# FoX attention block: the chunk factors of the softmax from four ScalarE activations instead of a GpSimd subtraction and one activation

## The chip, the cores and the metric

One core of a Trainium2 chip runs the whole program. The time is the device time of one execution in microseconds (us). The kernel before takes 590.53 us, the median of three runs (589.92 to 590.91). Lower is better.

The engines carry these names in the profile: PE is TensorE (matmuls and transposes), PEld its weight load, DVE is VectorE, ACT is ScalarE, POOL is GpSimd, SP only starts transfers. Each engine takes its instructions in order, and an instruction that waits holds up everything behind it on its engine.

## The reference

The input is 1024 positions of width 1024, with 16 learned positions put ahead of them (1040 in all). One layer does this, in float32:

```python
u    = rmsnorm(h, norm_g)
proj = u @ w_in     # q, k, v, forget logit, SiLU gate z, and four 512-wide parts of a convolution branch
c    = cumsum(log_sigmoid(f_logit + b_f))
s[t, j] = q_t . k_j / 8 + c[t] - c[j]   for j <= t, else -inf       # 8 heads of 64
attn = softmax(s) @ v
y    = concat(group_rmsnorm(attn) * silu(z), group_rmsnorm(gate_b * conv3(gate_c * xc)) * silu(z_conv))
out  = rmsnorm(h + y @ w_out, final_norm_g)[16:]
```

The change concerns the softmax. A row of scores is handled in two or three chunks of keys. Each chunk is exponentiated against its own maximum and summed; later each chunk is multiplied by exp(chunk maximum - row maximum) / (row sum).

## The kernel before

Float32 matmuls are done as three matmuls on split operands (high times high, low times high, high times low); `whi`/`wlo`, `ph`/`pl` and the like are such pairs. The first 160 us hold the projections to q, k, v and the forget logits. From about 160 to 490 us two streams are woven together on PE: the attention of eight heads, and as filler the remaining projection blocks (line 165, tile `pj`). From 490 us comes the output projection (line 788).

Each head is done in two halves of four 128-row query tiles: the narrow half (`c` = 0, tiles 0 to 3, up to 528 keys) and the wide half (`c` = 1, tiles 4 to 7, up to 1040 keys). For a half:

- `s_step` (lines 597 to 614), once per query tile and chunk: PE makes scores in `pn` (lines 605, 606); DVE takes the negated chunk maximum into `nmx` (line 612, or line 609 with the causal mask); ACT writes exp(score - maximum) into the SBUF tile `pn` of the row, with the sum into `smx` (line 613).
- `s_end` (lines 616 to 636), once per half, so 16 times: DVE reduces `nmx` to `mx`, the negated row maximum (619). POOL forms `mx - nmx` (621) and ACT exponentiates it (622): these are the factors `e`, 12 numbers in each of the 128 rows. POOL makes the row sums (624, 626, 627), DVE their reciprocal (628), POOL the final factors `fc` (630), and then multiplies each chunk of `pn` by its factor (635), nine pieces in a wide half and five in a narrow one.
- `t_step` (638 to 660): PE transposes 128-key slices of `pn` into `pt` (645); for slices on the diagonal DVE also fills a 32-wide corner (649, 651). ACT copies `pt` to `ph` (654), DVE makes the remainder `pl` (115).
- `v_step` (669): PE multiplies `ph` and `pl` by the values into `po`; `fold` (680, 681) takes them out.

The first transposes of a half need the first chunk of all four query tiles, that is the first four pieces of line 635. I number the 16 executions of `s_end` in order of time: odd ones end a wide half, even ones a narrow half. End 1 is at 177 us, end 3 at 216, end 7 at 295, end 9 at 336, end 10 at 354, end 11 at 375 and end 15 at 454.

The filler blocks each need a 128 x 1024 weight tile split in two: POOL copies `wm` to `wmhi` (line 112), and DVE makes `wmlo` from both (line 115). `wmhi` has two buffers, so a copy can start only when PE has read the last of the block before the present one.

The matmuls of the woven part are held in program order (`pinned`). All else is ordered by a scheduler that runs a timeline model over the program, so a change of one instruction's modelled time or engine can move others on ACT, DVE and POOL.

Of the kernel before, what the change touches and what calls it, by code (L numbers as in the profile page):

```python
# [11 lines left out]
AF = mybir.ActivationFunctionType  # L12
ALU = mybir.AluOpType
# [4 lines left out]
P = 128  # L18
# [17 lines left out]
def hybrid_kernel(ctx, tc, hT, h, w_q, w_vf, w_m, w_o, gn, bf, cw, ga, gc, gf, out):  # L36
    nc = tc.nc
# [141 lines left out]
    with ExitStack() as ca:  # L179
# [73 lines left out]
        for b in range(3):  # L253
            pr = psx.tile([P, 512], F32, name="px")
            w = 512 if b < 2 else NM
            for i in range(4 if b < 2 else 1):
                j = 4 * b + i
# [311 lines left out]
    nmx, smx = [], []  # L569
# [46 lines left out]
    def s_end(c):  # L616

        mx = pnp.tile([P, 4], F32, name="mx")
        nc.vector.tensor_reduce(mx, nmx[c], AX.X, ALU.min)
        e = pnp.tile([P, 4, 3], F32, name="e")  # L620
        nc.gpsimd.tensor_tensor(e, mx.unsqueeze(2).broadcast_to([P, 4, 3]), nmx[c], ALU.subtract)
        nc.scalar.activation(e, e, AF.Exp)
        t = pnp.tile([P, 4, 3], F32, name="t")
        nc.gpsimd.tensor_mul(t, e, smx[c])
        s = pnp.tile([P, 4], F32, name="s")
        nc.gpsimd.tensor_add(s, t[:, :, 0], t[:, :, 1])
        nc.gpsimd.tensor_add(s, s, t[:, :, 2])
        nc.vector.reciprocal(s, s)
        fc = pnp.tile([P, 4, 3], F32, name="fc", bufs=2)
        nc.gpsimd.tensor_mul(fc, e, s.unsqueeze(2).broadcast_to([P, 4, 3]))  # L630
        for i in range(3):
            for j in range(4 * c, 4 * c + 4):
                if i < len(SCH[j]):
                    k0, w = SCH[j][i]
                    nc.gpsimd.tensor_scalar(pn[j][:, k0:k0 + w], pn[j][:, k0:k0 + w], fc[:, j % 4, i:i + 1], 1.0,  # L635
                                            ALU.mult, ALU.mult)
# [79 lines left out]
    for g in range(-1, 2 * HEADS):  # L716
        steps = []
        if g >= 0 and g % 2 == 0 and g // 2 + 1 < HEADS:
            steps.append((0.0, 0.0, lambda hd=g // 2 + 1: load_head(hd)))
        if g + 1 < 2 * HEADS:  # L720
            hd, c = (g + 1) // 2, g % 2
            todo = [(2 * SCH[j][i][1] / 2400.0, lambda hd=hd, j=j, i=i: s_step(hd, j, i))
                    for j in range(4 * c, 4 * c + 4) for i in range(len(SCH[j]))]
            lo, hi = S_AT[g % 2 if g >= 0 else 2]
            spread(steps, todo, lo, hi)
            steps.append((hi, WAIT[g % 2 if g >= 0 else 2], lambda c=c: s_end(c)))
        if g >= 0:
            hd, c = g // 2, 1 - g % 2
            box = {}
            tv = []  # L730
            nk = 4 * c + 5
            for kt in range(nk + V_LAG):
                if kt < nk:
                    w = 512 - max(0, (kt - 4 * c) * P - 32)
                    tv.append((w / 1200.0, lambda c=c, kt=kt, box=box: t_step(c, kt, box)))
                if kt >= V_LAG:
                    w = 512 - max(0, (kt - V_LAG - 4 * c) * P - 32)
                    tv.append((w / 1200.0, lambda hd=hd, c=c, kt=kt - V_LAG, box=box: v_step(hd, c, kt, box)))
            spread(steps, tv, T_AT[c], V_END)
            steps.append((0.99, 0.0, lambda hd=hd, c=c, box=box: fold(hd, c, box)))  # L740
            if g > 0 and (g - 1) % 4 >= 2:
                steps.append((0.05, SOON, lambda m=(g - 1) // 4, c=g % 2: finish_soon(m, c)))
        stages.append([(x, s) for _, x, s in sorted(steps, key=lambda t: t[0])])
# [164 lines left out]
```

## Time and profile before

| | |
|---|---|
| median of 3 runs | 590.53 us |
| profiled execution | 590.42 us, its span 588.6 us, granted PE clock 0.998 |
| PE busy | 575.7 us, 98% of the span |
| PEld busy | 508.9 us, 86% |
| DVE busy | 373.5 us, 63% |
| ACT busy | 285.3 us, 48% |
| POOL busy | 145.2 us, 25% |

Busy time is the sum of an engine's instruction times without overlaps. The span runs from the first instruction to the last; about 1.8 us of the execution's time lie outside it. A number in square brackets at the end of a row of the timeline is the idle time of the engine just before that instruction, with what released it. Matmuls overlap, and their ends are modelled, so a wait of PE shows fully only when it is longer than this overlap; a wait of PEld shows when the weights for the next matmul could be loaded.

### The profile page before, as it was taken

What the parts mean: (1) busy time and instruction counts of PE and PEld (TensorE: products, weight loads), DVE (VectorE), ACT (ScalarE), POOL (GpSimd) and SP (SyncE); (2) the same over time, 40 slices, a digit from 0 to 9 for tenths busy, and PEclk for the clock granted to TensorE, in tenths of its full rate; (3) what the DMA queues carried; (4) which work ended last, traced back from release to release, by engine and by line L of the source; (5) the groups of instructions that cost most, each with busy time, mean ns of one, the idle gap of its engine ahead of it and who ended that gap; (6) DMA issues with size and microseconds to landing.
All of it is one profiled execution on the core that took longest, in us unless ns stands there. A gap on an engine that the chain in (4) does not pass through costs nothing.

```text
span 588.6 us, 9150 instructions
## 1 busy us (share of the span) xinstructions
PE 575.7 (98%) x3230; PEld 508.9 (86%) x3230; DVE 373.5 (63%) x842; ACT 285.3 (48%) x667; POOL 145.2 (25%) x282
## 2 busy tenths in 40 slices
PE   9999999999998999999999999999999999999995
PEld 6889999999997889997879997888997878888884
DVE  5515951133356786879876878876879768847342
ACT  5354431131043574565763755756645657815231
POOL 1102010121027234242263155350531520000000
PEclk9999999999999999999999999999999999999999
DMA  8664694249811514514326126152251045743201
GB/s 296 215 223 135 207 339 139 71 144 282 257 53 37 146 36 116 141 59 114 86 77 145 55 94 146 63 130 66 80 211 37 1 162 225 240 161 128 88 36 71
DMA packets 35221, 78.14 MB, mean 133 GB/s; under 512 B 4024, under 2 KB 13384, under 8 KB 35176
## 3 DMA queue, kind: packets, MB, share of 16 engines
q1 hardware_dynamic: 35032, 77.57, 42.1%
q8 instruction: 25, 0.41, 0.3%
q14 instruction: 20, 0.16, 0.1%
q10 hardware_dynamic: 144, 0.00, 0.0%
HBM read 55.92 MB, written 21.64 MB: 132 GB/s over the span
## 4 chain that ended last, share of the span: by engine, by line
PE 83%; DVE 5%; DMA 4%; POOL 4%; ACT 2%; issue 1%; SPq 0%; POOLq 0%; ACTq 0%; DVEq 0%
PE pj L165 30%; PE p L788 10%; PE ps L324 8%; PE ps L232 7%; PE po L669 5%; PE pj L788 5%; PE pt L645 5%; PE ps L165 4%; DMA k<-kd 3%; PE pn L605 3%; PE pn L606 3%; POOL pn L635 1%; DMA wm<-in_w_m 1%; DVE wmlo L115 1%; PE px L232 1%
## 5 line engine op out<-in xcount | busy, mean ns | idle before, releaser
L165 PE MATMUL pj<-xhi,wmhi 128*128 128x512 f32 (+1 forms) x384 | 145.0, 377 | 0.9 <-DVE kf L275 0.6
L165 PE MATMUL pj<-xhi,wmlo 128*128 128x512 f32 (+1 forms) x384 | 137.1, 357 | 0.0
L165 PE MATMUL pj<-xlo,wmhi 128*128 128x512 f32 (+1 forms) x384 | 136.9, 357 | 0.0
L613 ACT ACTIVATE pn<-pn,nmx 128x328 f32<-128x328 f32 (+6 forms) x112 | 60.6, 542 | 52.6 <-DVE nmx L612 27.6
L165 PEld LDWEIGHTS pj<-xhi,wmlo 128*128 128x128 f32 x384 | 72.2, 188 | 8.4
L165 PEld LDWEIGHTS pj<-xhi,wmhi 128*128 128x128 f32 x384 | 72.6, 189 | 6.2 <-issue 1.3
L165 PEld LDWEIGHTS pj<-xlo,wmhi 128*128 128x128 f32 x384 | 72.8, 190 | 3.8
L654 ACT CAST ph<-pt 128x512 fp32r<-128x512 f32 (+4 forms) x112 | 49.6, 446 | 50.1 <-PE po L669 23.1
L635 POOL TENSOR_SCALAR pn<-pn,fc 128x328 f32<-128x328 f32 (+4 forms) x112 | 69.5, 642 | 1.6
L115 DVE TENSOR_TENSOR pl<-pt,ph 128x512 fp32r<-128x512 f32 (+1 forms) x96 | 54.6, 572 | 19.5 <-ACT ph L654 18.7
L112 POOL TENSOR_SCALAR wmhi<-wm 128x1024 fp32r<-128x1024 f32 x24 | 26.5, 1102 | 139.6 <-DMA wm<-in_w_m 80.4
L645 PE MATMUL pt<-ident,pn 128*128 128x128 f32 x288 | 47.4, 273 | 3.3 <-POOL pn L635 1.5
L645 PEld LDWEIGHTS pt<-ident,pn 128*128 128x128 f32 x288 | 36.3, 140 | 13.7 <-POOL pn L635 2.8
L115 DVE TENSOR_TENSOR wmlo<-wm,wmhi 128x1024 fp32r<-128x1024 f32 x24 | 30.2, 1260 | 17.9 <-POOL wmhi L112 17.9
L609 DVE CUSTOM_DVE_ANT_0 pn<-pn,maskn 128x328 f32<-128x328 f32 (+3 forms) x64 | 31.9, 500 | 10.9 <-PE pn L606 9.2
L669 PE MATMUL po<-ph,v 128*128 128x512 f32 (+4 forms) x112 | 37.0, 336 | 0.4 <-DVE ph L115 0.4
L605 PE MATMUL pn<-k,q 128*128 128x328 f32 (+6 forms) x112 | 36.6, 328 | 0.0
L606 PE MATMUL pn<-k,q 66*128 66x328 f32 (+6 forms) x112 | 36.1, 322 | 0.0
L669 PE MATMUL po<-pl,v 128*128 128x512 f32 (+1 forms) x96 | 33.3, 350 | 0.0
L165 PE MATMUL ps<-xhi,wmhi 128*128 128x346 f32 (+1 forms) x96 | 30.9, 322 | 0.0
L612 DVE TENSOR_REDUCE nmx<-pn 128x1 f32<-128x346 f32 (+4 forms) x48 | 24.8, 521 | 9.5 <-PE pn L606 9.5
L165 PE MATMUL ps<-xlo,wmhi 128*128 128x346 f32 (+1 forms) x96 | 30.8, 321 | 0.0
(227 smaller groups left out, 1198.1 us busy)
## 6 DMA issues: line engine op xcount, KB each, us to landing
wm<-in_w_m SPq DMA_DIRECT2D x24, 512.0 KB, 3.7
k<-kd SPq DMA_DIRECT2D x24, 260.0 KB, 5.4
q<-qd SPq DMA_DIRECT2D x24, 256.0 KB, 5.8
vd<-vv SPq DMA_DIRECT2D x9, 512.0 KB, 2.9
v<-vd SPq DMA_DIRECT2D x8, 576.0 KB, 6.6
ht<-in_h SPq DMA_DIRECT2D x8, 512.0 KB, 6.0
yd<-gy SPq DMA_DIRECT2D x16, 256.0 KB, 2.8
q<-in_w_o SPq DMA_DIRECT2D x8, 512.0 KB, 3.4
```

The source lines that it names most:

```text
L115: nc.vector.tensor_tensor(lo, src, f(hi), ALU.subtract)
L165: ins = nc.tensor.matmul(ps[:, :w], wt[:, k, :], xt[:, t0:t0 + w], start=(k == 0 and n == 0), stop=(k == KT - 1 and n == 2))
L232: nc.tensor.matmul(psq[m][c], wt[:, m * P:(m + 1) * P], xt[:, NM + 512 * c:NM + 512 * c + 512], start=(k == 0 and n == 0), stop=(k == KT - ...
L324: nc.tensor.matmul(ps[c][:P if n == P else 48, :260], x[k][:, ts_] if n == P else x[:, k, :], w[k][:, 260 * c:260 * c + 260], start=(k == ...
L605: pinned(nc.tensor.matmul(ps[:, :w], q1[:, qs], k1[:, ks], start=True, stop=False))
L606: pinned(nc.tensor.matmul(ps[:, :w], q2[:DH + 2, qs], k2[:DH + 2, ks], start=False, stop=True))
L613: nc.scalar.activation(pn[j][:, ks], ps[:, :w], AF.Exp, bias=nmx[c][at], scale=-1.0 if last else 1.0, accum_out=smx[c][at])
L635: nc.gpsimd.tensor_scalar(pn[j][:, k0:k0 + w], pn[j][:, k0:k0 + w], fc[:, j % 4, i:i + 1], 1.0, ALU.mult, ALU.mult)
L645: pinned(nc.tensor.transpose(pt[:, q0:q0 + P], pn[j][:, ks], ident))
L654: nc.scalar.copy(ph[:, at:], pt[:, at:])
L669: pinned(nc.tensor.matmul(po[:, at:], v2[:, vk, :], t[:, at:], start=(kt == 0 and i == 0), stop=(kt == 4 * c + 4 and i == len(parts) - 1)))
L788: ins = nc.tensor.matmul(held[n][:, :w], a[:, tt], b[:, cs], start=(e == ORDER[0] and i == 0), stop=(e == ORDER[-1] and i == 2))
```

## The change

The subtraction on POOL is gone. ACT computes exp(-1 * nmx + mx) straight away; since the bias of an activation is one number per row, there is one activation for each of the four query tiles, over its three chunks.

```diff
         e = pnp.tile([P, 4, 3], F32, name="e")
-        nc.gpsimd.tensor_tensor(e, mx.unsqueeze(2).broadcast_to([P, 4, 3]), nmx[c], ALU.subtract)
-        nc.scalar.activation(e, e, AF.Exp)
+        for j in range(4):
+            nc.scalar.activation(e[:, j, :], nmx[c][:, j, :], AF.Exp, bias=mx[:, j:j + 1], scale=-1.0)
```

Over the program POOL has 16 instructions fewer and ACT 48 more. The order of instructions on PE and of transfers on SP stays as it was. ACT, DVE and POOL have some places where neighbours change their order. Three of them follow.

POOL at end 15, before: the row sum (`s`), the final factors (`fc`), nine pieces of `pn`, then the split of the next block's weights (`wmhi`).

```order
L627 TENSOR_TENSOR s<-s,t 128x4
L630 TENSOR_TENSOR fc<-e,s 128x12
L635 TENSOR_SCALAR pn_1620<-pn_1620,fc 128x328
L635 TENSOR_SCALAR pn_1621<-pn_1621,fc 128x392
L635 TENSOR_SCALAR pn_1622<-pn_1622,fc 128x456
L635 TENSOR_SCALAR pn_1623<-pn_1623,fc 128x346
L635 TENSOR_SCALAR pn_1620<-pn_1620,fc 128x328
L635 TENSOR_SCALAR pn_1621<-pn_1621,fc 128x392
L635 TENSOR_SCALAR pn_1622<-pn_1622,fc 128x456
L635 TENSOR_SCALAR pn_1623<-pn_1623,fc 128x346
L635 TENSOR_SCALAR pn_1623<-pn_1623,fc 128x348
L112 TENSOR_SCALAR wmhi<-wm 128x1024
```

POOL at end 15, now:

```order
L624 TENSOR_TENSOR t<-e,smx_1629 128x12
L626 TENSOR_TENSOR s<-t 128x4
L627 TENSOR_TENSOR s<-s,t 128x4
L112 TENSOR_SCALAR wmhi<-wm 128x1024
L630 TENSOR_TENSOR fc<-e,s 128x12
L635 TENSOR_SCALAR pn_1620<-pn_1620,fc 128x328
L635 TENSOR_SCALAR pn_1621<-pn_1621,fc 128x392
L635 TENSOR_SCALAR pn_1622<-pn_1622,fc 128x456
L635 TENSOR_SCALAR pn_1623<-pn_1623,fc 128x346
```

The weight split has moved from behind the nine pieces to a place ahead of the final factors. Its partner on DVE (`wmlo`) has moved forward as well, to just behind the remainder `ph` 32x32 of this half.

DVE at end 9, before: the reciprocal `s` (628) among the corner fills of `pt`, the remainders `pl` and the take-out of a filler block (`cx`, 457).

```order
L416 TENSOR_TENSOR gy<-gy,cv 128x512
L649 MEMSET pt 128x32
L115 TENSOR_TENSOR pl<-pt,ph 128x288
L417 SCALAR_TENSOR_TENSOR gy<-gy,gct,zc 128x512
L651 STREAM_TRANSPOSE pt<-pn_1618 32x32
L649 MEMSET pt 128x32
L628 RECIPROCAL s<-s 128x4
L651 STREAM_TRANSPOSE pt<-pn_1619 32x32
L457 TENSOR_TENSOR cx<-pj,cx 128x342
L115 TENSOR_TENSOR pl<-pt,ph 128x160
L115 TENSOR_TENSOR ph<-pt,ph 32x32
```

DVE at end 9, now:

```order
L416 TENSOR_TENSOR gy<-gy,cv 128x512
L649 MEMSET pt 128x32
L417 SCALAR_TENSOR_TENSOR gy<-gy,gct,zc 128x512
L651 STREAM_TRANSPOSE pt<-pn_1618 32x32
L115 TENSOR_TENSOR pl<-pt,ph 128x288
L457 TENSOR_TENSOR cx<-pj,cx 128x342
L115 TENSOR_TENSOR pl<-pt,ph 128x160
L628 RECIPROCAL s<-s 128x4
L649 MEMSET pt 128x32
L651 STREAM_TRANSPOSE pt<-pn_1619 32x32
L115 TENSOR_TENSOR ph<-pt,ph 32x32
```

The reciprocal, and with it the last corner fill, now stand behind `cx` and the remainder `pl` 128x160.

DVE at end 7, before: the weight remainder `wmlo`, then the reciprocal and the remainder `pl` 128x160.

```order
L115 TENSOR_TENSOR wmlo<-wm,wmhi 128x1024
L649 MEMSET pt 128x32
L628 RECIPROCAL s<-s 128x4
L115 TENSOR_TENSOR pl<-pt,ph 128x160
L651 STREAM_TRANSPOSE pt<-pn_1619 32x32
L436 SCALAR_TENSOR_TENSOR otmp<-zs,otmp 128x512
```

DVE at end 7, now:

```order
L115 TENSOR_TENSOR wmlo<-wm,wmhi 128x1024
L649 MEMSET pt 128x32
L115 TENSOR_TENSOR pl<-pt,ph 128x160
L628 RECIPROCAL s<-s 128x4
L651 STREAM_TRANSPOSE pt<-pn_1619 32x32
L436 SCALAR_TENSOR_TENSOR otmp<-zs,otmp 128x512
```

The reciprocal has moved one place back, behind `pl` 128x160.

## Rows read from the trace of the kernel before

**Rows 1.** Windows: stretch, us; busy us (instructions) of PE, PEld, DVE, ACT, POOL.

```profile
160.00:490.00 330.00, 325.96 (x1821) 287.29 (x1821) 253.25 (x612) 191.95 (x486) 123.25 (x220) 1.00 0.32 93
490.00:581.60 91.60, 91.60 (x422) 75.65 (x420) 51.56 (x102) 38.06 (x80) 0.00 (x0) 1.00 0.40 145
```

**Rows 2.** Waits of PE: line waited for, us in total, times, longest us.

```profile
PE pt L645 <- POOL pn L635: 1.5, 1, 1.5
```

**Rows 3.** Groups of ACT by shape: busy us, mean ns of one.

```profile
L622 ACT ACTIVATE e<-e 128x12 f32<-128x12 f32 x16 | 3.5, 216 | 3.5 <-POOL e L621 3.5
L804 ACT ACTIVATE gy<-k 128x512 f32<-128x512 f32 x9 | 5.6, 627 | 21.4 <-DVE k L801 21.4
L814 ACT ACTIVATE k<-k,r 128x512 f32<-128x512 f32 x5 | 3.6, 718 | 1.8 <-DVE r L89 1.8
```

**Rows 4.** Timeline at end 3: start us, us, instruction, [idle before <-releaser].

```profile
215.81 0.17 DVE L619 TENSOR_REDUCE mx<-nmx 128x4 f32<-128x12 f32 x1
216.06 0.21 POOL L621 TENSOR_TENSOR e<-mx,nmx 128x12 f32<-128x12 f32 x1 [7.81 <-DVE mx L619]
216.63 0.21 POOL L624 TENSOR_TENSOR t<-e,smx 128x12 f32<-128x12 f32 x1 [0.36 <-ACT e L622]
```

**Rows 5.** Timeline at end 15, engine by engine.

```profile
455.29 0.22 ACT L622 ACTIVATE e<-e 128x12 f32<-128x12 f32 x1
457.39 2.78 POOL L635 TENSOR_SCALAR pn<-pn,fc 128x328 f32<-128x328 f32 x4
463.36 1.05 POOL L112 TENSOR_SCALAR wmhi<-wm 128x1024 fp32r<-128x1024 f32 x1
457.03 0.39 PE L165 MATMUL pj<-xlo,wmhi 128*128 128x512 f32 x1
458.63 0.27 PE L669 MATMUL po<-ph,v 128*128 128x32 f32 x1
458.37 0.19 DVE L115 TENSOR_TENSOR ph<-pt,ph 32x32 fp32r<-32x32 f32 x1
460.22 0.42 PEld L645 LDWEIGHTS pt<-ident,pn 128*128 128x128 f32 x4 [0.27 <-POOL pn L635]
```

**Rows 6.** Timeline at end 7, engine by engine.

```profile
297.28 1.28 POOL L627 TENSOR_TENSOR s<-s,t 128x4 f32<-128x4 f32 x1
297.28 1.23 DVE L115 TENSOR_TENSOR wmlo<-wm,wmhi 128x1024 fp32r<-128x1024 f32 x1
298.60 0.18 DVE L628 RECIPROCAL s<-s 128x4 f32<-128x4 f32 x1
301.92 0.42 PEld L645 LDWEIGHTS pt<-ident,pn 128*128 128x128 f32 x4 [0.28 <-POOL pn L635]
```

**Rows 7.** Timeline at end 9, engine by engine.

```profile
338.27 0.32 PE L165 MATMUL pj<-xhi,wmlo 128*128 128x342 f32 x1
340.00 0.22 PE L669 MATMUL po<-ph,v 128*128 128x32 f32 x1
338.22 0.18 DVE L628 RECIPROCAL s<-s 128x4 f32<-128x4 f32 x1
338.68 0.52 DVE L457 TENSOR_TENSOR cx<-pj,cx 128x342 f32<-128x342 f32 x1
339.11 0.32 DVE L115 TENSOR_TENSOR pl<-pt,ph 128x160 fp32r<-128x160 f32 x1
339.46 0.19 DVE L115 TENSOR_TENSOR ph<-pt,ph 32x32 fp32r<-32x32 f32 x1
```

**Rows 8.** Timeline at end 10, engine by engine.

```profile
354.63 1.24 POOL L621 TENSOR_TENSOR e<-mx,nmx 128x12 f32<-128x12 f32 x1
356.09 1.28 DVE L462 SCALAR_TENSOR_TENSOR cv<-cx,cwt,cv 128x1024 f32<-128x1024 f32 x1
358.03 0.18 DVE L628 RECIPROCAL s<-s 128x4 f32<-128x4 f32 x1 [0.66 <-POOL s L627]
358.93 0.30 PE L645 MATMUL pt<-ident,pn 128*128 128x128 f32 x1 [0.64 <-DVE pl L115]
```

## The prediction

> **What bounds the kernel now.** I read the busy times by stretch first, then the waits of PE, then the timeline around each `s_end`. In the woven part PE is busy for 325.96 of 330 us, and from 490 us to the last matmul for all of 91.60 us [rows 1]. So the time is PE's work plus some 4 us of waits in the woven part. The change leaves PE's work and its order alone; it can only take some of those waits away or add new ones, and no later idle time is there to swallow an added one. The reader should see in the rows that the work on `s_end` reaches PE in one way: the first four pieces of line 635 must be done before the first transposes of a half. The longest wait of PE on them is 1.5 us, once, at end 1 [rows 2]. At ends 7 and 15 the weight load waited 0.28 and 0.27 us for them [rows 5, 6], which PE's overlap hides almost wholly: there is no slack left at these two, and what comes later there costs PE the same.
>
> **The chain itself.** At end 3, where ACT was free, 0.82 us passed from the start of `mx` to the start of `t` (216.63 - 215.81). Of this 0.25 us led up to the subtraction, and the remaining 0.57 held the subtraction (0.21), the activation (0.22) and two handoffs, so about 0.07 each [rows 4]. In the new chain the 0.25 and one handoff stay, and four activations stand between. The old one took 216 ns for 12 numbers a row [rows 3]: that is the lower bound of a new one. It had no operand of one number per row; of two 512-wide activations the one with such an operand takes 718 ns against 627 [rows 3], so 0.09 us more, and 0.31 is the upper bound. Neither row is nearer (one has the size, the other the operand), so I take 0.25 us. Four are 1.0 us (0.86 to 1.24), and the chain is 1.32 us against 0.82: 0.5 us longer (0.36 to 0.74), not shorter. The 64 activations add 16.0 - 3.5 = 12.5 us to ACT, which is busy 191.95 of the 330 us [rows 1]; ACT does not become the bound.
>
> The Trainium skill speaks against this step too (ScalarE: Activation LUTs, section "ACT is a hardware spline evaluator"): an activation whose bias is one number per row takes about 280 ns before its first element. By it four would be an estimated 1.13 us and the chain 0.63 us longer. No row of this kernel has this form at this size, and the sum does not use the figure.
>
> **Where the chain has cover.** At the ends not named below PE showed no wait on the pieces [rows 2], so the extra 0.5 us is hidden by the time between the fourth piece and the transposes. If that cover is short at one of the wide ends, it costs up to 0.5 us there; I count 0.1 us for all of them (0 to 0.6). At end 1 PE already waits, so the chain's change would count in full: between -0.3 us (POOL is spared an instruction) and +0.5 us. I take 0.
>
> **End 15, where POOL's order changes.** This is the main term. The split of the next block's weights (`wmhi`) now stands ahead of the final factors. It ran at 463.36 us behind all nine pieces and takes 1.05 us. It cannot run before PE has started and finished the last matmul on the buffer it overwrites, at 457.03 + 0.39 = 457.42 us [rows 5]. So it ends at about 458.5 us, then the final factors need 0.3 us with handoffs, and the four pieces start at 458.8 us instead of 457.39: 1.4 us later. If the buffer comes free as the matmul starts, it is 1.0 us. On top of that `wmlo` on DVE follows `wmhi` closely in the new order. At end 7 a POOL sum over four numbers a row took 1.28 us beside a `wmlo` of 1.23 us that began with it [rows 6]: POOL stood still until DVE was done. If all of such a standstill falls onto the four pieces, the delay is 2.6 us. The 2.78 us of the four pieces [rows 5] may already hold part of another one, so I add only 0.2 us and take 1.6 us (1.0 to 2.6). ACT's longer chain is not added: ACT reached `e` at 455.29 us [rows 5], and another 0.8 us there still ends before the wait for the buffer does. DVE's `ph` 32x32, which PE used at 458.63 us, 0.07 us after its end (458.37 + 0.19) [rows 5], will be late as well behind DVE's new order; that stall lies inside the same delay and is not counted twice.
>
> **End 7, where the reciprocal moves behind `pl` 128x160.** Before, it started at 298.60 us, just after `wmlo` ended (297.28 + 1.23 = 298.51) [rows 6], so the longer chain is hidden by `wmlo`. The instruction now ahead of it takes 0.32 us in the same shape at end 9 [rows 7]. With no slack at the transposes (301.92 us) [rows 6] that is 0.3 us; if the chain is not hidden, 0.8. I take 0.4 us.
>
> **End 9, where it moves behind `cx` and `pl` 128x160.** `cx` reads what PE ended at 338.27 + 0.32 = 338.59 us, so the reciprocal comes after 338.59 + 0.52 + 0.32 = 339.43 us, against 338.22 [rows 7]: 1.2 us later. Behind it stand the last corner fill and so `ph` 32x32, which began 1.24 us after the reciprocal; 0.84 of this was `cx` and `pl`, so at least 0.40 us remain, and it ends at 340.02 us at the earliest. PE wanted it at 340.00 us, 0.35 us after its old end (339.65) [rows 7]. The stall is between 0 and 1.2 - 0.35 = 0.85 us; I take 0.5 us.
>
> **End 10, a gain.** The subtraction took 1.24 us here, the reciprocal then waited 0.66 us for POOL, and PE waited 0.64 us for a remainder `pl` that stood behind the reciprocal on DVE [rows 8]. With the subtraction gone the sums can move forward, but they must still find their way past a DVE product of 1.28 us [rows 8], so not the whole 0.64 us comes back: I take 0.3 us (0 to 0.64).
>
> **The sum.** 1.6 + 0.4 + 0.5 + 0.1 - 0.3 = 2.3 us, on the profiled execution's 590.42 us: 592.7 us. That execution stands 0.1 us under the median of the runs, so the forecast of the median is the same within a tenth. 0.2%, about what a measurement of this kernel can tell from no change, is 1.2 us: faster is below 589.3 us, slower above 591.7.
>
> **Rivals.**
>
> *The standstill decides (slower still).* `wmlo` begins ahead of the four pieces and POOL stands still for all of it. For it: the 1.28 us beside 1.23 [rows 6]. Against it: `wmlo` stands behind four other DVE instructions in the new order and may come only when the pieces are half done. End 15 then costs 2.6 us, the sum is 3.3 us and the time 593.7 us; with the upper ends at 7 and 9 it is 594.4. The Trainium skill has this rule (SBUF — State Buffer, section "SBUF: two separate sides"): DVE with two SBUF inputs and GpSimd take a shared port in turn, and the later one is blocked wholly. The rows at end 7 agree.
>
> *The new order costs little (no change).* The delay at end 15 is at its lower end, 1.0 us, ends 7 and 9 lose 0.3 and 0.1 us because DVE finds the same gaps as before, and end 10 gains 0.6: the sum is 0.8 us, 591.2 us. For it: most of these delays depend on a few tenths of slack. Against it: the buffer's release at 457.42 us is PE's own time and cannot move forward.
>
> *POOL's relief decides (faster).* The subtraction was an instruction on an engine that DVE holds up, as the 1.24 us show [rows 8]. If the chain without it passes DVE's long products in a gap, PE's 1.5 us at end 1 [rows 2] shrinks by half and the 0.64 us at end 10 go, some 1.4 us together, 589.0 us. It needs end 15 to cost nothing, that is, the weight split to begin before about 456.1 us, 1.3 us ahead of the pieces' old start. PE's matmul at 457.03 us [rows 5] speaks against it.
>
> **How the numbers follow.** The forecast has 0.52 (591.8 to 594.0), the standstill 0.12, no change 0.27, faster 0.09. Slower is 0.52 + 0.12 = 0.64. The range of 590.8 to 594.4 us leaves out the faster case and the lower part of no change, some 0.15, and little above.
>
> **What would show it.** In the changed kernel's profile: activations of 3 numbers a row at 0.22 to 0.31 us; `wmhi` near 457.5 us (plus what PE lost before) with the final factors right behind it, and a wait of PE on the `pn` pieces, or on `ph` just before, of 1.0 to 2.6 us at end 15, none like it before; at end 9 a wait of PE on `ph` of up to 0.85 us; at end 10 a wait on `pl` under 0.64 us. I am wrong if PE shows no wait at end 15, if the four activations take under 0.8 us together and the waits at end 1 shrink, or if PE's busy time itself changes.

## The result: slower by 5 us, beyond the range forecast

The changed kernel takes 595.75 us (median of six runs, 595.13 to 596.83); the kernel before took 590.56 beside it (six runs, 588.97 to 592.05). The ratio is 1.0085, 95% interval 1.0072 to 1.0099, so about 5.0 us more. The forecast was 592.7 us (590.8 to 594.4). The profiled execution took 596.62 us, its span 594.9 us with a mean granted clock of 0.992.

The windows of the changed kernel, for the stretches that answer to [rows 1] (the second view is the same, cut around end 15; columns as there, the last three being the granted clock, DMA share and GB/s):

```profile
160.00:496.00 336.00, 328.25 (x1818) 289.67 (x1819) 252.32 (x612) 201.81 (x534) 123.12 (x204) 0.99 0.31 91
496.00:588.00 92.00, 91.89 (x423) 75.93 (x421) 51.89 (x103) 38.32 (x80) 0.00 (x0) 1.00 0.41 145
...
456.00:470.00 14.00, 11.22 (x45) 9.30 (x46) 8.36 (x20) 7.50 (x20) 8.97 (x14) 0.76 0.00 0
```

The woven part is 6 us longer. PE idles for 336 - 328.25 = 7.75 us of it, where it was 4.04 [rows 1]: 3.7 us of new waits. The other 2.3 us are in its busy time; over the whole program that is 578.2 us where it was 575.7, for 3230 matmuls in both. The third row shows where: in the 14 us around end 15 PE was busy for 11.22 us, at a mean clock of 0.76.

The waits of PE, over the whole program (answers to [rows 2]):

```profile
PE pt L645 <- POOL pn L635: 4.5, 3, 2.2
...
PE po L669 <- DVE ph L115: 1.2, 2, 0.7
PE pt L645 <- DVE pl L115: 1.1, 2, 0.7
```

Waits on the pieces of line 635 were one of 1.5 us; now there are three, 4.5 us together: 1.51 at end 1 as before, 0.78 at end 7, and 2.19 at end 15.

The timeline at end 15, engine by engine (answers to [rows 5]):

```profile
458.45 1.46 POOL L112 TENSOR_SCALAR wmhi<-wm 128x1024 fp32r<-128x1024 f32 x1 [0.33 <-PE pj L165]
459.88 0.20 POOL L630 TENSOR_TENSOR fc<-e,s 128x12 f32<-128x12 f32 x1
460.18 3.77 POOL L635 TENSOR_SCALAR pn<-pn,fc 128x328 f32<-128x328 f32 x4
460.18 1.62 POOL L635 TENSOR_SCALAR pn<-pn,fc 128x328 f32<-128x328 f32 x1
...
458.30 0.72 DVE L438 TENSOR_TENSOR zc<-zc,otmp 128x512 f32<-128x512 f32 x1
460.03 0.19 DVE L115 TENSOR_TENSOR ph<-pt,ph 32x32 fp32r<-32x32 f32 x1
460.25 1.22 DVE L115 TENSOR_TENSOR wmlo<-wm,wmhi 128x1024 fp32r<-128x1024 f32 x1
...
460.27 0.28 PE L669 MATMUL po<-ph,v 128*128 128x32 f32 x1 [0.53 <-DVE ph L115]
464.00 1.12 PE L645 MATMUL pt<-ident,pn 128*128 128x128 f32 x4 [2.19 <-POOL pn L635]
```

The weight split waits for PE's buffer, as forecast, and the final factors come 1.43 us behind its start. Then the four pieces take 3.77 us instead of 2.78 [rows 5]; the first alone (fourth row) takes 1.62 us, beside a `wmlo` of 1.22. PE stands still from 461.81 to 464.00 us (464.00 less the idle 2.19). Windows of 2 us over the same stretch show what follows:

```profile
462.00:464.00 2.00, 0.00 (x0) 0.00 (x0) 0.91 (x3) 1.02 (x5) 2.00 (x4) 0.71 0.00 0
464.00:466.00 2.00, 2.00 (x7) 1.81 (x8) 0.22 (x1) 0.84 (x2) 2.00 (x4) 0.50 0.00 0
466.00:468.00 2.00, 2.00 (x7) 1.51 (x7) 1.26 (x2) 0.28 (x1) 0.72 (x2) 0.50 0.00 0
468.00:470.00 2.00, 2.00 (x8) 1.71 (x7) 0.69 (x1) 1.17 (x2) 0.00 (x0) 0.59 0.00 0
470.00:472.00 2.00, 2.00 (x13) 1.66 (x13) 1.18 (x3) 1.06 (x3) 0.00 (x0) 1.00 0.00 0
```

While PE stood still the granted clock went from 2.4 to 1.2 GHz (0.50), at 462.83 us, and came back at 469.65: for the 5.65 us from 464.00 on PE ran 7 or 8 instructions in 2 us, and 13 once the clock was back. Nothing of the kind was in the kernel before in this part [rows 1].

Set beside each other matmul by matmul, the starts of PE in the two profiled executions drift apart like this (worked out from both traces): 0.94 us up to end 15, 0.70 us at its `po`, 2.14 us at its transposes, 2.48 us in the slow matmuls after; 6.25 us together.

The activations, by shape (answers to [rows 3]) and at end 3, and the rows at ends 7, 9 and 10 (answers to [rows 6 to 8]), from the changed kernel:

```profile
L622 ACT ACTIVATE e<-nmx,mx 128x3 f32<-128x3 f32 x64 | 14.3, 290 | 1.5 <-DVE mx L619 1.1 <-DVE pt L649 0.2
...
216.49 0.84 ACT L622 ACTIVATE e<-nmx,mx 128x3 f32<-128x3 f32 x4
```

```profile
298.13 1.22 DVE L115 TENSOR_TENSOR wmlo<-wm,wmhi 128x1024 fp32r<-128x1024 f32 x1
299.58 0.16 DVE L628 RECIPROCAL s<-s 128x4 f32<-128x4 f32 x1
300.12 4.24 POOL L635 TENSOR_SCALAR pn<-pn,fc 128x328 f32<-128x328 f32 x6
303.33 0.66 PE L645 MATMUL pt<-ident,pn 128*128 128x128 f32 x4 [0.78 <-POOL pn L635]
...
340.26 0.17 DVE L628 RECIPROCAL s<-s 128x4 f32<-128x4 f32 x1
341.09 0.19 DVE L115 TENSOR_TENSOR ph<-pt,ph 32x32 fp32r<-32x32 f32 x1 [0.31 <-ACT ph L654]
...
357.96 1.28 DVE L462 SCALAR_TENSOR_TENSOR cv<-cx,cwt,cv 128x1024 f32<-128x1024 f32 x1
359.34 0.18 DVE L628 RECIPROCAL s<-s 128x4 f32<-128x4 f32 x1
```

One activation takes 290 ns, but each starts some 0.19 us behind the one before it, and the four at end 3 took 0.84 us together. PE showed a new wait at end 7, none at end 9, and the one of end 10 is gone. New waits that belong to no end of the forecast are two of 0.68 us at end 6 and one of 0.43 us at 349 us, between ends 9 and 10.

### The profile page after: what moved, and what is told of

The parts are those of the page before. It is cut to its first block, busy times and chain, and to the rows that moved or that the text cites. A ratio compares the mean times of both kernels' runs of the same rounds, so it can differ in the third digit from the quotient of the medians.

```text
span 594.9 us, 9267 instructions
## 1 busy us (share of the span) xinstructions
PE 578.2 (97%) x3230; PEld 511.4 (86%) x3230; DVE 372.6 (63%) x842; ACT 295.1 (50%) x715; POOL 144.0 (24%) x266
## 4 chain that ended last, share of the span: by engine, by line
PE 84%; DMA 4%; DVE 4%; POOL 4%; issue 2%; ACT 1%; SPq 0%; POOLq 0%; ACTq 0%; DVEq 0%
PE pj L165 31%; PE p L788 10%; PE ps L324 8%; PE ps L232 7%; PE po L669 5%; PE pt L645 5%; PE pj L788 5%; PE ps L165 4%; DMA k<-kd 3%; PE pn L605 3%; PE pn L606 3%; POOL pn L635 2%; DMA wm<-in_w_m 1%; DVE wmlo L115 1%; PE px L232 1%
```

## The experiments

**1. The split goes back.** The changed kernel, with the weight split of end 15 held behind the ninth piece. `after(ins, name)` has the scheduler place `ins` behind the instruction `name`.

```diff
-        hi_pool(whi, ws)
+        ins = hi_pool(whi, ws)
+        if len(ends) == 15:
+            after(ins, last_piece[0])
...
```

> The changed kernel, with the weight split wmhi of end 15 put back behind the nine pieces; the four activations and every other change of order stay. Theory (the moved split costs the time: 2.2 us of waiting for the pieces and some 2.1 us of half clock after it): 4.3 us come back, 591.4 us, no row at half clock between 160 and 490 us. Rival 1 (the longer chain on ACT costs the time, spread over 16 ends): under 1 us comes back, 595 us.

Measured: 592.25 us (ten runs, 591.16 to 593.82), the kernel before beside it 591.27; ratio 1.0012 (0.9996 to 1.0027). Waits of PE in this kernel:

```profile
PE pt L651 <- POOL pn L639: 2.3, 2, 1.5
```

Two waits on the pieces are left (ends 1 and 7); the one at end 15 is gone, and its windows show a clock of 1.00. This one move carries 0.0085 - 0.0012 = 0.0073 by the ratios, 4.3 us of the 5.0. The rival that ACT's longer chain is the cause falls: the four activations are all in this kernel. They can have a share only in the 0.7 us that are left (up to 1.6 by the interval).

**2. The split alone.** The kernel before, its chain untouched, with the split of end 15 ahead of the final factors.

```diff
+        def pieces(name=None):
+            ins = nc.gpsimd.tensor_mul(fc, e, s.unsqueeze(2).broadcast_to([P, 4, 3]))
+            if name:
+                after(ins, name)
...
-        hi_pool(whi, ws)
+        ins = hi_pool(whi, ws)
         lo_vec(wlo, ws, whi)
+        if held_back:
+            held_back.pop()(ins.ins.name)
```

> The kernel before (subtraction on POOL, one activation), with only the weight split of end 15 put ahead of the final factors. Theory: PE waits about 2 us for the pieces, the granted clock falls to half for some us after it; 594.5 us (593.5 to 595.5). Rival 1 (chain on ACT): no change, 590.5 us.

Measured: 595.73 us (five runs), ratio 1.0066 (1.0049 to 1.0084). PE's row at end 15 of this kernel, and windows there:

```profile
468.61 1.12 PE L659 MATMUL pt<-ident,pn 128*128 128x128 f32 x4 [2.88 <-POOL pn L644]
```

```profile
466.00:468.00 2.00, 0.00 (x0) 0.00 (x0) 1.34 (x5) 1.69 (x6) 2.00 (x4) 0.84 0.01 4
468.00:470.00 2.00, 1.39 (x6) 1.30 (x7) 0.13 (x1) 0.24 (x1) 2.00 (x4) 0.50 0.00 0
...
472.00:474.00 2.00, 2.00 (x8) 1.72 (x7) 0.21 (x1) 0.80 (x2) 0.00 (x0) 0.50 0.00 0
474.00:476.00 2.00, 2.00 (x12) 1.69 (x12) 1.66 (x4) 0.92 (x3) 0.00 (x0) 0.95 0.00 0
```

Without any of the four activations such a wait (2.88 us in one, where the changed kernel had 0.53 and 2.19) and the same half clock appear, and most of the loss with them (3.9 us by ratio). The profiled execution of this kernel took 601.28 us, its longest: PE also stood for 2.46 us up to 53.12, where nothing had been edited, and the granted clock was 0.50 from 54.34 to 57.76. So the span of this execution says nothing of the edit; the median of the five runs does.

**3. PE kept at work.** The changed kernel, with 18 bf16 matmuls on the identity put ahead of the waiting transposes of end 15; the transposes write over their results. The condition holds at the first transposes of the eighth wide half, that is end 15.

```diff
...
+        if sum(wide) == 8 and wide[-1]:
+            idb = ident.bitcast(BF16)
+            for _ in range(18):
+                pinned(nc.tensor.matmul(pt[:, :256], idb[:, :P], idb, start=True, stop=True))
```

> The changed kernel, with 18 small matmuls of no use put on PE just ahead of the transposes of end 15 that wait, so that PE works while it waits (about 2 us of work). Theory (the half clock comes from PE standing still): the clock stays full, the wait itself stays, about 2.1 us come back, 593.6 us. Rival 2 (the half clock has another cause, or its rows cost nothing): 595.7 us or more, clock row at 0.5 as before.

Measured: 595.05 us (four runs), ratio 1.0058 (1.0043 to 1.0073). PE at end 15, and the windows, of this kernel:

```profile
462.06 2.14 PE L649 MATMUL pt<-ident 128*128 128x256 bf16 x18
464.42 0.66 PE L652 MATMUL pt<-ident,pn 128*128 128x128 f32 x4 [0.21 <-POOL pn L635]
```

```profile
464.00:466.00 2.00, 1.79 (x11) 1.41 (x10) 1.16 (x2) 0.87 (x2) 2.00 (x4) 1.00 0.00 0
466.00:468.00 2.00, 2.00 (x13) 1.73 (x12) 1.46 (x3) 0.89 (x2) 1.55 (x3) 1.00 0.00 0
468.00:470.00 2.00, 2.00 (x15) 1.65 (x14) 0.79 (x3) 1.11 (x3) 0.00 (x0) 1.00 0.00 0
```

The transposes start as late as before (3.74 us behind the `po` ahead of them, 3.73 in the changed kernel), but the clock stays at 2.4 GHz. That is worth 594.9 - 592.7 = 2.2 us by the spans and 0.0027, 1.6 us, by the ratios: the half clock is a cost of its own, behind the wait. Expected was a gain of 2.1 us on the 595.75; the ratios' intervals hold that too. The other runs agree: the mean granted clock was 0.992 to 0.995 in the six of the changed kernel, and 0.997 or 0.998 in the four of this one. The profiled execution of the changed kernel is among the lowest (0.992), which may be why its trace shows a larger loss than the ratios.

**4. `wmlo` out of the way.** The changed kernel, the split still ahead of the final factors, with `wmlo` held behind the first remainder `pl` of the half.

```diff
-        lo_vec(wlo, ws, whi)
+        if len(ends) == 15:
+            held_back.append(lambda: lo_vec(wlo, ws, whi))
+        else:
+            lo_vec(wlo, ws, whi)
...
-            lo_vec(pl[:, at:], pt[:, at:], ph[:, at:])
+            ins = lo_vec(pl[:, at:], pt[:, at:], ph[:, at:])
+            if held_back:
+                after(held_back.pop()(), ins.ins.name)
```

> The changed kernel with wmhi left ahead of the final factors, but wmlo on DVE held until after the first transposes of the half. Theory: POOL's pieces no longer stand still beside wmlo, PE's wait for the pieces shrinks from 2.2 to about 1.0 us; if a wait of that length leaves the clock alone, as the 1.5 us at end 1 did, the half clock goes too: 592.4 us. If the clock falls all the same, 594.5 us. Rival 1 (chain on ACT): 595.7 us.

Measured: 593.91 us (five runs), ratio 1.0045 (1.0027 to 1.0063). POOL and PE at end 15:

```profile
460.75 2.26 POOL L640 TENSOR_SCALAR pn<-pn,fc 128x328 f32<-128x328 f32 x4
...
463.06 0.66 PE L651 MATMUL pt<-ident,pn 128*128 128x128 f32 x4 [0.69 <-POOL pn L640]
```

The four pieces take 2.26 us instead of 3.77, PE's wait is 0.69 instead of 2.19, and the clock stays at 1.00 (the mean of the whole execution is 0.996 to 0.998 in all five runs). So the standstill beside `wmlo` costs 1.5 us, and without it PE's wait is short enough to leave the clock alone. By the ratios the gain is 2.4 us, by the spans 3.2 (594.9 to 591.7), where 3.3 was expected; the ratios' intervals hold that too.

**5. POOL's sums at end 1, in the kernel before.** One rival had the time fall because POOL is spared a subtraction. These are POOL's rows at end 1 in the changed kernel, and two of DVE:

```profile
175.59 2.19 POOL L460 TENSOR_SCALAR cv<-cx,cwt 128x1024 f32<-128x1024 f32 x1
177.92 1.24 POOL L624 TENSOR_TENSOR t<-e,smx 128x12 f32<-128x12 f32 x1
179.24 1.23 POOL L626 TENSOR_TENSOR s<-t 128x4 f32<-128x4 f32 x1
180.55 0.20 POOL L627 TENSOR_TENSOR s<-s,t 128x4 f32<-128x4 f32 x1
181.04 1.09 POOL L630 TENSOR_TENSOR fc<-e,s 128x12 f32<-128x12 f32 x1 [0.29 <-DVE s L628]
...
177.81 1.28 DVE L461 SCALAR_TENSOR_TENSOR cv<-cx,cwt,cv 128x1024 f32<-128x1024 f32 x1 [0.86 <-POOL cv L460]
180.88 1.19 DVE L463 TENSOR_TENSOR cv<-cv,rbc 128x1024 f32<-128x1024 f32 x1
```

The subtraction is gone, but the sums and the factors `fc`, 0.2 us long elsewhere, stand still beside DVE's 1024-wide products of lines 461 to 463. The experiment holds line 460, and with it these products, behind the fourth piece:

```diff
-                nc.gpsimd.tensor_scalar(cv, cx[:, 2:1026], cwt[:, i, 2:3], 1.0, ALU.mult, ALU.mult)
+                def conv(name=None):
+                    ins = nc.gpsimd.tensor_scalar(cv, cx[:, 2:1026], cwt[:, i, 2:3], 1.0, ALU.mult, ALU.mult)
+                    if name:
+                        after(ins, name)
...
+        if conv_late:
+            conv_late.pop()(fourth[0])
```

> The kernel before, with the four operations on cv of the first filler block (lines 460 to 463) held until the fourth piece of end 1 has been issued on POOL. Theory (at end 1 POOL's own short sums are held by DVE's 1024-wide products: 0.90, 1.23 and 1.10 us for instructions that take 0.2 us elsewhere, and the 2.2 us cv on POOL runs right ahead of them): the sums take 0.2 us each, PE's 1.54 us wait at end 1 goes, and the time falls by 1.5 us, to 589.1 us where the kernel before has 590.6. Rival (PE's wait there ends on the four pieces themselves, or the held products collide with end 2 and give it back there): 590.6 us, with a new wait of PE between 190 and 200 us.

Measured: 589.1 us (nine runs, 588.18 to 590.47), the kernel before beside it 591.09; ratio 0.9972 (0.9957 to 0.9987). POOL at end 1 of this kernel:

```profile
176.60 0.21 POOL L636 TENSOR_TENSOR t<-e,smx 128x12 f32<-128x12 f32 x1 [0.32 <-ACT e L634]
176.89 0.20 POOL L638 TENSOR_TENSOR s<-t 128x4 f32<-128x4 f32 x1
177.17 0.20 POOL L639 TENSOR_TENSOR s<-s,t 128x4 f32<-128x4 f32 x1
177.66 0.21 POOL L642 TENSOR_TENSOR fc<-e,s 128x12 f32<-128x12 f32 x1 [0.29 <-DVE s L640]
```

PE's 1.54 us wait at end 1 is gone, and no wait over 0.10 us took its place in the next 60 us. This version is faster than both kernels, by 1.65 us against the kernel before. The hold takes two things away from end 1 at once, DVE's products and POOL's own `cv` of line 460. From `mx` to the first piece it is 3.3 us shorter than in the kernel before: 2.6 us in the sums and in `fc`, which stood beside the products, and 0.7 us ahead of the subtraction, which had waited for `cv`. The two were not tried apart.

**6. The same hold in the changed kernel**, with the split of experiment 1 held as well.

> The changed kernel with the weight split of end 15 held behind the ninth piece (as in the run that undid that move) and the same hold of cv at end 1. Theory: the wait of 1.5 us at end 1 goes as in the run beside it; what stays against the kernel before are waits of 0.68, 0.68, 0.78 and 0.51 us at ends 6, 7 and 15, less the 0.64 at end 10: 1.5 us under the run without the hold, that is 0.8 us under the kernel before (589.8 where that has 590.6). If the longer chain on ACT matters at end 1 once the products are gone, PE keeps a wait of up to 0.6 us there and the gain is 0.9 us only.

Measured: 591.25 us (twelve runs), ratio 1.0002 (0.9986 to 1.0017). Waits of PE:

```profile
PE po L689 <- DVE ph L117: 1.2, 2, 0.7
PE pt L665 <- DVE pl L117: 1.1, 2, 0.7
...
PE pt L665 <- POOL pn L649: 0.8, 1, 0.8
```

The wait at end 1 is gone here too, longer chain or not. Between the runs 5 and 6, alike but for the change without its move at end 15, lie 0.0030, 1.8 us. PE's idle time behind 162 us, all of it waits, is 3.72 us here and 2.49 in run 5, 1.23 us more; the rest is within the intervals. So what is left of the change, the other reorderings and the longer chain together, costs about 1.2 us, and experiment 1's interval, 0.9996 to 1.0027, holds that value as well. I had expected 0.8 us under the kernel before here, and it is level with it. Against experiment 1 the hold is worth 0.0010, 0.6 us, where 1.5 was expected; the intervals hold both. Which of the moves on DVE makes the waits at ends 6, 7 and 15 was not tried one by one. At end 6 DVE's new order shows where they can come from: `pl` 128x416 now stands behind line 472, and `ph` 32x32 behind line 438, both ahead of these lines before.

## Why the forecast was wrong

- **The step that failed is the end of the sum: a wait was priced at its own length.** End 15 was put at 1.6 us and nothing behind it. PE's wait was followed by 6.8 us of half clock, 2.5 us in the trace and 1.6 us by experiment 3's ratio. No term and no rival had this. The prediction did name a change of PE's busy time as a sign of being wrong, and it came, 2.3 us in the woven part. With the wait kept and the clock full, experiment 3's ratio gives an estimated 590.53 x 1.0058 = 594.0 us, inside the range: the half clock took the time out of it.
- **End 15 itself was under-sized, 2.84 us (0.70 + 2.14) for 1.6.** Its place and its mechanism were right: experiments 1 and 2 show that the moved split decides. The 0.70 is a wait on `ph` by DVE's new order, which stays in experiment 1 (0.51 us); in experiment 2, without that order, the pieces alone cost 2.88, so it lies inside the same delay, as forecast. The two parts of this delay are off. The delay by the split was put at 1.4 us. The pieces began at 460.18; the old start with PE's drift is 457.39 + 0.94 = 458.33, so 1.85: `wmhi` took 1.46 us, beside DVE's line 438, and not 1.05. The standstill was put at 0.2 us and is 3.77 - 2.78 = 0.99 against before, 1.5 against experiment 4. The rival "the standstill decides" had this term nearly right (2.6 us); I gave it 0.12 and stayed near the lower end because `wmlo` stood behind four DVE instructions, which only decided that it began 0.07 us after the first piece instead of earlier. By the Trainium skill's rule for the port that DVE and GpSimd share (SBUF — State Buffer, section "SBUF: two separate sides") the later one waits for the whole of the other. The trace agrees on the size, as the first piece took 1.62 us where it takes 0.54 in experiment 4, but not on the order: the piece had begun 0.07 us before the `wmlo` of 1.22 us.
- **The chain.** One activation takes 290 ns, between the bounds and above the 250 taken. The Trainium skill states about 280 ns before the first element for an activation whose bias is one number per row (ScalarE: Activation LUTs, section "ACT is a hardware spline evaluator"); the trace agrees. But the prediction added the four end to end, 1.0 us, and they overlap: 0.84 us at end 3, 0.85 to 0.86 at nine other ends, up to 1.4 where other work of ACT comes between. From `mx` to `t` the new chain took 1.20 us at end 13, where ACT was free, against 0.77 before: 0.4 us longer, within the forecast's 0.36 to 0.74. In the queues of the other ends it was between 0.6 us shorter (end 10) and 1.4 us longer (end 8). It cost nothing that shows at end 15, where the split waited for PE and not for the chain (the 0.33 us in its row), nor at end 1 in experiment 6.
- **Ends 6, 7, 9 and 10.** End 7 was put at 0.4 us; PE's drift there is 0.64, and the row on the pieces is 0.78 us. But the reciprocal came only some 0.2 us later than in [rows 6], once PE's drift of 0.8 is taken off (299.58 - 298.60 - 0.8); what is longer is the first four pieces behind it, 3.16 us where they took 2.71. End 9 was put at 0.5 us and cost nothing: with PE's drift of 1.38 taken off, the reciprocal came 0.66 us later than in [rows 7] and not 1.2. The prediction had `cx` read what the matmul at 338.27 leaves; with the drift that one began at 339.66, and `cx` at 339.61, so it reads something earlier. And `ph` 32x32 ended at 341.28, before 340.00 + 1.38 = 341.38. End 10 was put at -0.3 and gave -0.70, its whole wait. Two waits of 0.68 us at end 6 and one of 0.43 at 349 us had no term, and an old one of 0.80 at 266 us, before end 6, went. The forecast had 0.7 us for all these; the trace has 0.83 (the drift of 0.94 less the 0.11 that was there at 160 us): the sum was right by luck, as most of its parts were not.
- **"POOL's relief decides"** had the right engine and the wrong instruction. Experiment 5 shows that POOL's chain at end 1 is held in the main by DVE's products, which removing one short instruction does not move.

## What to carry to other kernels

When PE is the bound, a new wait of some us has two prices: its length, and what the granted clock takes back afterwards; look up in the trace whether waits of that size were followed by half clock. When a change lets a scheduler move a long instruction ahead of short ones that PE waits for, count its partner on the other engine too, and the standstill between the two. Before taking work off an engine, see whether its short instructions are long because of it, or because of another engine's.

## What the hardware showed that was not expected

The wait of 1.51 us at end 1 (up to 184.56) left the clock at 1.00, as these windows of the changed kernel show; so did 0.54 and 0.69 us 2 us apart in experiment 4.

```profile
182.00:184.00 2.00, 1.05 (x6) 0.70 (x5) 1.47 (x6) 1.23 (x4) 1.90 (x5) 1.00 0.00 0
184.00:186.00 2.00, 1.44 (x10) 1.26 (x11) 0.12 (x1) 1.03 (x3) 2.00 (x4) 1.00 0.00 0
```

The waits of 2.19 us (the changed kernel), 2.88 and 2.46 us (experiment 2) were each followed by half clock, for 6.83, 6.83 and 3.4 us, although PE was busy again from the end of the wait on. The clock fell 1.02 us after PE had stopped in the changed kernel (461.81 to 462.83); in experiment 2 it fell 1.63 us after the stop at 465.73, and 3.68 us after the one at 50.66, when PE was at work again. So these cases show no fixed delay between the stop and the fall. Why it differs, and the length of the half clock with it, stays open.
